# Next block's output projection ahead of a block's last feed-forward group

## The chip, the cores and the metric

The kernel runs on one core of one Trainium2 chip. The metric is the device time of one execution in microseconds (us), lower is better. The engines of the core are PE (TensorE, matrix multiplication, with its weight load PEld), DVE (VectorE), ACT (ScalarE), POOL (GpSimd) and SP (SyncE, which issues nearly all DMAs). Each engine works through its own instructions in order and waits on semaphores for the others.

## What is computed

One decoder layer over 2048 new tokens (one sequence, d_model 1024) and 8 sample tokens with carried states. Two head groups, RWKV-7 and Mamba-2, mix tokens; their outputs, side by side, go through `w_out`; two DeepNorm LayerNorms surround a squared-ReLU feed-forward of width 4096. Cut to the part that the change touches:

```python
proj = x @ w_in                                   # 1024 -> input of both mixers
o_r, wkv_fin = rwkv7_mix(...)                     # 512 columns
o_m, ... = mamba2_mix(...)                        # 512 columns
mix = jnp.concatenate([o_r, o_m], -1) @ w_out     # the output projection
h = layer_norm(ALPHA * x + mix, ln1_g, ln1_b, LN_EPS)
ff = jnp.square(jax.nn.relu(h @ w_ff1)) @ w_ff2
y = layer_norm(ALPHA * h + ff, ln2_g, ln2_b, LN_EPS)
```

Results are float32 within a tight tolerance, so each large product is done as three matmuls on a high and a low half of each factor.

## The kernel before

The 2048 tokens are four blocks of `TB` = 512. First `project` runs x @ w_in for all blocks (to about 760 us), with the mixers of the early blocks beside it. Then `tail(b)` runs once per block, in this order: output projection; first LayerNorm; transposes to `hT` (token columns, feature rows); then 8 groups g of the feed-forward. A group is four `ff1` (one slice f of 128 hidden features each, `LA` = 3 slices run ahead) and 8 units of the second product, one for each half of the output columns (`dh`) and each tile i of 128 tokens. One such unit is 12 matmuls of 512 columns.

A weight piece is made by `wpiece` (L201): SP reads 256 KB into a `wr` tile, ACT rounds it to the high half (L198), DVE or POOL subtracts for the low half (L199). There are 7 `wr` and 8 `w` tiles. `mm3` (L163 to L168) issues the three matmuls: high by high (L166), high by low (L167), low by high (L168). In the traces psb and psa are the four large accumulation banks, psm a small one. The wide tiles (4 KB per partition, names g) hold a block's four h tiles, the hidden slices and the gains; there are 12.

The output projection of a block works in halves of two token tiles. Each half goes through w_out in quarters q of 256 columns; three of four quarters are loaded again for the second half, in turned order, so a block reads 28 pieces. After each bank, L1309 adds it to the residual h, and L1205 takes statistics. `ln` (L1207) finishes the norm: a dozen small DVE instructions, then one ACT instruction per tile (L1222). `gain` multiplies and adds the norm's parameters (L1227, L1228, 128x1024 on DVE). The norm's gains of the first LayerNorm for the transposed copy are folded into L1347, which brings the transposes (`tr`, L173) out of their bank. The first four slices of ff1 (`FIRST`) run over the first 256 tokens while the second half's norm is made.

What a block still owes when its last group ends (second norm, its gains, the store of y) is kept in `late` and stepped by the next block's output projection, two steps per token tile in its second half.

`drive` runs a tail and, for each unit's worth of time that the tail yields, gives a share to fills: the mixers of the next block (`RATE_M` 0.23; with the 8 sample tokens 0.35 in block 0). `before_last(b)`, called when the last group's four ff1 are issued, drains the fills and makes the next tail. That call contains `load_o` (L323), which reads the mixers' output back from DRAM (s_o, 8 pieces of 256 KB) and splits it into `act` tiles. The mixer's last piece, `rwkv_post`, ends in a chain: `inv_root` (a matmul with cst, then DVE), a broadcast through DRAM (d_rs: L552 writes, L554 reads), L786, the read of s_bv (L785), L788, L790, the gate (matmul qsg by gup), L797, and the write of s_o (L798). In before, the last group's units 1 to 7 alternate with the first units of the next projection.

Of the kernel before, what the change touches and what calls it, by code (L numbers as in the profile page):

```python
# [10 lines left out]
F32R = mybir.dt.float32r  # L11
I32 = mybir.dt.int32
AF = mybir.ActivationFunctionType
ALU = mybir.AluOpType
# [13 lines left out]
BUFS = (("wr", 7), ("w", 8), ("act", 8), ("g4", 12), ("r", 2), ("blk", 4),  # L28
        ("m2", 3), ("q2", 2), ("m4", 2), ("ms", 1), ("lr", 1), ("sc", 2), ("ar", 2), ("bk", 1), ("xs", 3),
        ("xf", 1), ("uv", 2), ("bt", 1), ("st", 2), ("r1", 1), ("hids", 8))  # L30
D = 1024
KT = 8
TB = 512
NS = 8
DFF = 4096
NFT = DFF // 128
ALPHA = 2.0 ** 0.25
# [71 lines left out]
class K:  # L109
# [122 lines left out]
    def setup_mix(self):  # L232
# [1045 lines left out]

    def tail(self, b, act, before_last):

        self.pf = "o"
        nc, A = self.nc, self.A
        smp = b == self.sblk
        bs = self.sm("bs", [128, 4, 2, 6], bufs=2)
        W = TB + (NS if smp else 0)
        hs = []
        ln = iter(())
        for half in range(2):
            it = (2 * half, 2 * half + 1)
            tok = smp and half == 1  # L1290
            for q in range(4) if half == 0 else range(3, -1, -1):
                qs = slice(q * 256, (q + 1) * 256)
                if half == 0 or q < 3:
                    wq = [self.wpiece(A["w_out"][q, kp], (2, 256)) for kp in range(4)]
                if len(hs) <= it[0]:
                    for i in it:
                        h = self.wide()
                        nc.sync.dma_start(h, A["x_p"][b * TB + i * 128:b * TB + (i + 1) * 128, :])
                        hs.append(h)
                    if tok:  # L1300
                        xs = self.wide()
                        nc.sync.dma_start(xs[0:8], A["x_s"])
                for i in it:
                    ps = self.bank((128, 256))
                    for k in range(KT):
                        l = [act[k][:, s, i * 128:(i + 1) * 128] for s in range(2)]
                        r = [wq[k // 2][s][:, k % 2, :] for s in range(2)]
                        self.mm3(ps, l, r, k == 0, k == KT - 1)
                    nc.vector.scalar_tensor_tensor(out=hs[i][:, qs], in0=hs[i][:, qs], scalar=ALPHA, in1=ps,  # L1309
                                                   op0=ALU.mult, op1=ALU.add)  # L1310
                    if (q % 2 == 1) != (half == 1):
                        self.stats(hs[i], bs[:, i], q // 2)
                    if half == 1:
                        next(ln, 0)
                        next(self.late, 0)
                    yield 2.6
                if tok:
                    ps = self.bank((128, 256))
                    for k in range(KT):
                        for s in range(2):  # L1320
                            self.mm(ps[0:16], self.osT[:, k, :], wq[k // 2][s][:, k % 2, :],
                                    k == 0 and s == 0, k == KT - 1 and s == 1)
                    nc.scalar.activation(xs[64:80, qs], ps[0:16], AF.Copy)
            for _ in ln:
                pass
            ln = self.ln([hs[i] for i in it], [bs[:, i] for i in it], 128)
            if tok:
                ln = itertools.chain(ln, self.ln_s(xs))
                hs.append(xs)
        for _ in self.late:  # L1330
            pass

        hT = []
        for half in range(2):
            for k in range(KT):
                if half == 0:
                    hT.append(self.sb("act", (128, 2, TB + NS), F32R))
                hl = hT[k]
                p = self.bank((128, 264))
                for i in range(2):  # L1340
                    self.tr(p[:, i * 128:(i + 1) * 128], hs[2 * half + i][:, k * 128:(k + 1) * 128])
                n = 256
                if smp and half == 1:
                    self.tr(p[:, 256:264], hs[4][0:8, k * 128:(k + 1) * 128])
                    n = 264
                raw = self.sb("r", (128, 512))[:, :n]
                nc.scalar.activation(raw, p[:, :n], AF.Identity, scale=self.par("g1", k), bias=self.par("b1", k))  # L1347
                o = 256 * half
                self.split(raw, hl[:, 0, o:o + n], hl[:, 1, o:o + n])
            if half == 0:  # L1350
                first = []
                for f in range(FIRST):
                    first.append(self.ff1(f, hT, [(0, 256)]))
                    next(ln, 0)
                    yield 2.6
                for _ in ln:
                    pass
        self.pf = "f"
        g1 = self.affine(1)
        gain = itertools.chain(*([self.gain(h, 128, *g1) for h in hs[:4]] +  # L1360
                                 ([self.gain(hs[4][0:8], 8, *g1)] if smp else [])))
        segs = [(0, 256), (256, 264)] if smp else [(0, 512)]
        done = {}
        for f in range(FIRST):
            done[f] = self.ff1(f, hT, [(256, W - 256)], first[f])
            next(gain, 0)
            yield 2.6

        def up(f):
            if f < NFT and f not in done:  # L1370
# [3 lines left out]
        nxt = None  # L1374
        for g in range(NFT // 4):
            for f in range(4 * g, 4 * g + 4 + LA):
                if up(f):
                    next(gain, 0)
                    yield 5.2
            for _ in gain:  # L1380
                pass
            hid = [done.pop(f) for f in range(4 * g, 4 * g + 4)]
            last = g == NFT // 4 - 1
            if last:
                nxt = before_last(b)
                self.pf = "f"
                bs = self.sm("bs", [128, 4, 2, 6], bufs=2)
                rows = [A["y_p"][b * TB + i * 128:b * TB + (i + 1) * 128, :] for i in range(4)]
            w2s = []
            order = [(dh, i) for dh in range(2) for i in range(4)]  # L1390
            if last and nxt is None:
                order = [(dh, i) for i in range(4) for dh in range(2)]
            for dh, i in order:
                ds_ = slice(dh * 512, dh * 512 + 512)
                if len(w2s) == dh:
                    w2 = [self.wpiece(A["w_ff2"][f * 128:(f + 1) * 128, ds_], (1, 512)) for f in range(4 * g, 4 * g + 4)]
                    w2s.append(w2)
                    if smp:
                        ps = self.bank()
# [11 lines left out]
                ps = self.bank()  # L1411
                for f in range(4):
                    l = [hid[f][0][:, s, i * 128:(i + 1) * 128] for s in range(2)]
                    r = [w2[f][s][:, 0, :] for s in range(2)]
                    self.mm3(ps, l, r, f == 0, f == 3)
                self.accum(hs[i][:, ds_], ps, g == 0)
                if last:
                    self.stats(hs[i], bs[:, i], dh)
                    if dh == 1 and i == 0:
                        ab = self.affine(2)  # L1420
                    if nxt is None and dh == 1:
                        self.norm(hs[i], bs[:, i], ab, rows[i], POOLN[i])
                    if nxt is not None and 4 * dh + i >= BESIDE:
                        self.pf = "o"
                        yield next(nxt)
                        self.pf = "f"
                yield 2.6

        def finish():
            if nxt is not None:  # L1430
                yield from self.ln(hs[:4], [bs[:, i] for i in range(4)], 128)
# [6 lines left out]
        self.late = finish()  # L1438
        self.nxt = nxt

    def ff1(self, f, hT, segs, hid=None):
# [66 lines left out]
def body(tc, A, nb=4):  # L1508
    with ExitStack() as es:
        k = K(tc, A, nb, es)  # L1510
# [15 lines left out]
        smp = [k.sample(), "s", k.sblk, RATE_S]  # L1526
# [14 lines left out]
        for b in range(nb):  # L1541
# [8 lines left out]
        for _ in k.late:  # L1550
            pass
        k.es2.close()


def layouts(x):

    ac = np.ascontiguousarray
    g = {n: np.asarray(a) for n, a in x.items()}
    d = {}
# [31 lines left out]
    d["w_out"] = ac(g["w_out"][0].reshape(4, 2, 128, 4, 256).transpose(3, 0, 2, 1, 4).reshape(4, 4, 128, 512))  # L1591
# [38 lines left out]
```

## Time and profile before

| what | us |
|---|---|
| median of 3 runs | 2873.99 (2873.67 to 2876.23) |
| profiled execution | 2874.12 |
| its span in the trace | 2872.3 |
| PE busy | 2764.3 (96%) |
| PEld busy | 2280.3 (79%) |
| DVE busy | 2028.7 (71%) |
| ACT busy | 1291.8 (45%) |
| POOL busy | 365.5 (13%) |
| DMA | 395.56 MB, 45.1% of 16 engines on the main queue |

PE is the engine to watch: it is idle for 108 us of the span, and its granted clock is 0.982 of full speed on average. The page's chain of waits that ended last is PE for 73%, DVE for 15% and DMA for 4%. A time lost by another engine counts where PE has to wait for it.

### The profile page before, as it was taken

The numbers are of one execution on the slowest core, as the hardware profiler recorded it, in microseconds if no ns is written. First come the engines' busy times: TensorE is split into PE (matmuls) and PEld (weight loads), VectorE is DVE, ScalarE is ACT, GpSimd is POOL, SyncE is SP. The second block draws the span as 40 slices with busy tenths as digits, with TensorE's granted clock in tenths as the row PEclk, the third lists the DMA queues.
The fourth block names the chain that finished last, engine by engine and source line by source line (L and its number), as shares of the span: only waits on it lengthen the run. The fifth ranks groups of instructions, "written<-read, shape, count | busy, mean of one in ns | idle before, by whom it ended". The sixth has DMA issues, their size and how long they took to land.

```text
span 2872.3 us, 52296 instructions
## 1 busy us (share of the span) xinstructions
PE 2764.3 (96%) x19066; PEld 2280.3 (79%) x19066; DVE 2028.7 (71%) x4809; ACT 1291.8 (45%) x2510; POOL 365.5 (13%) x508
## 2 busy tenths in 40 slices
PE   9998999899989999999899999998999999899997
PEld 7798887677878777778788888887777778888886
DVE  7878969878878776766867667568767656754446
ACT  5554544445527343434544444336344333543432
POOL 2222222212221000002200000022000001200001
PEclk9999999999999999999999999999999999899999
DMA  6655555556644444445434434354443435433231
GB/s 204 190 179 142 174 163 141 166 162 185 197 130 156 126 122 122 136 134 185 144 96 123 121 105 128 92 185 130 125 133 113 115 102 171 151 107 94 86 103 70
DMA packets 333766, 395.56 MB, mean 138 GB/s; under 512 B 84990, under 2 KB 191060, under 8 KB 333500
## 3 DMA queue, kind: packets, MB, share of 16 engines
q1 hardware_dynamic: 333508, 392.22, 45.1%
q8 instruction: 150, 2.46, 0.4%
q14 instruction: 108, 0.88, 0.1%
HBM read 331.34 MB, written 60.81 MB: 137 GB/s over the span
## 4 chain that ended last, share of the span: by engine, by line
PE 73%; DVE 15%; DMA 4%; issue 4%; ACT 2%; SPq 1%; POOL 0%; DVEq 0%; ACTq 0%; POOLq 0%
PE psb L166 17%; PE psb L167 16%; PE psb L168 16%; PE psm L152 6%; PE psa L166 4%; PE psa L167 4%; PE psa L168 4%; DVE w L199 2%; PE psc L152 2%; DVE lr L665 1%; PE psm L173 1%; DVE rX L666 1%; PE psy L751 1%; PE psa L152 1%; DMA wr<-in_w_ff_dram 1%
## 5 line engine op out<-in xcount | busy, mean ns | idle before, releaser
L198 ACT ACTIVATE w<-wr 128x512 fp32r<-128x512 f32 (+1 forms) x836 | 516.5, 626 | 571.7 <-PE psb L168 191.6
L199 DVE TENSOR_TENSOR w<-wr,w 128x512 fp32r<-128x512 f32 x712 | 512.5, 726 | 226.6 <-ACT w L198 221.1
L166 PE MATMUL psb<-act,w 128*128 128x512 f32 (+2 forms) x1768 | 627.3, 356 | 6.4 <-ACT act L198 5.7
L167 PE MATMUL psb<-act,w 128*128 128x512 f32 (+2 forms) x1768 | 620.7, 352 | 0.2 <-DVE act L199 0.2
L168 PE MATMUL psb<-act,w 128*128 128x512 f32 (+2 forms) x1768 | 617.2, 350 | 2.3 <-DVE w L199 2.3
L166 PEld LDWEIGHTS psb<-act,w 128*128 128x128 f32 x1768 | 336.6, 191 | 56.4 <-ACT act L198 5.9
L168 PEld LDWEIGHTS psb<-act,w 128*128 128x128 f32 x1768 | 336.1, 190 | 47.9 <-DVE w L199 2.7
L167 PEld LDWEIGHTS psb<-act,w 128*128 128x128 f32 x1768 | 337.3, 191 | 43.7 <-DVE act L199 1.3
L166 PE MATMUL psb<-w,g 128*128 128x512 f32 x788 | 315.3, 401 | 2.3 <-ACT w L198 1.4
L167 PE MATMUL psb<-w,g 128*128 128x512 f32 x788 | 312.7, 397 | 0.2 <-DVE w L199 0.2
L168 PE MATMUL psb<-w,g 128*128 128x512 f32 x788 | 310.8, 395 | 0.0
L199 POOL TENSOR_TENSOR w<-wr,w 128x512 fp32r<-128x512 f32 x124 | 185.9, 1504 | 530.9 <-ACT w L198 414.6
L1505 DVE TENSOR_TENSOR g<-psb,g 128x512 f32<-128x512 f32 x173 | 118.8, 688 | 148.5 <-PE psb L168 148.1
L166 PEld LDWEIGHTS psb<-w,g 128*128 128x128 f32 x788 | 148.0, 188 | 39.8 <-ACT w L198 2.2
L168 PEld LDWEIGHTS psb<-w,g 128*128 128x128 f32 x788 | 147.9, 188 | 34.3 <-DVE g L199 0.2
L167 PEld LDWEIGHTS psb<-w,g 128*128 128x128 f32 x788 | 148.3, 188 | 33.1 <-DVE w L199 0.5
L199 DVE TENSOR_TENSOR g<-r,g 128x256 fp32r<-128x256 f32 (+1 forms) x172 | 96.7, 562 | 84.6 <-ACT g L198 83.6
L1455 ACT ACTIVATE r<-psb 128x512 f32<-128x512 f32 (+2 forms) x130 | 63.4, 489 | 199.3 <-PE psb L168 197.6
L166 PE MATMUL psa<-act,w 128*128 128x256 f32 (+2 forms) x336 | 115.8, 345 | 0.0
L167 PE MATMUL psa<-act,w 128*128 128x256 f32 (+2 forms) x336 | 114.3, 340 | 0.0
L168 PE MATMUL psa<-act,w 128*128 128x256 f32 (+2 forms) x336 | 113.8, 339 | 0.0
L167 PE MATMUL psb<-w,act 128*128 128x256 f32 x352 | 101.8, 289 | 6.4 <-DVE w L199 5.4
(376 smaller groups left out, 5204.1 us busy)
## 6 DMA issues: line engine op xcount, KB each, us to landing
wr<-in_w_ff_dram SPq DMA_DIRECT2D x512, 256.0 KB
wr<-in_w_in_dram SPq DMA_DIRECT2D x208, 256.0 KB
wr<-in_w_out_dram SPq DMA_DIRECT2D x112, 256.0 KB
lr<-d_l SPq DMA_DIRECT2D x256, 64.0 KB
s_m<-g SPq DMA_DIRECT2D x48, 256.0 KB
ms<-s_m SPq DMA_DIRECT2D x16, 768.0 KB
wr<-in_xT_dram SPq DMA_DIRECT2D x32, 256.0 KB
s_ar<-g SPq DMA_DIRECT2D x16, 512.0 KB
```

Of the source, the lines that this page charges most:

```text
L152: return self.nc.tensor.matmul(out, l, r, start=start, stop=stop)
L166: nc.tensor.matmul(out, l[0], r[0], start=first, stop=False)
L167: nc.tensor.matmul(out, l[0], r[1], start=False, stop=False)
L168: nc.tensor.matmul(out, l[1], r[0], start=False, stop=last)
L173: self.nc.tensor.transpose(out, in_, self.cst[p0:p0 + k, o + p0:o + p0 + k])
L198: nc.scalar.activation(hi, raw, AF.Copy)
L199: (eng or nc.vector).tensor_tensor(out=lo, in0=raw, in1=hi.bitcast(F32), op=ALU.subtract)
L665: nc.vector.tensor_tensor(out=row, in0=X[:, :, s + 1:16], in1=row, op=ALU.mult)
L666: nc.vector.tensor_reduce(X[:, :, s:s + 1], lr[:, :, 17 * s:16 * s + 16], axis=AX.X, op=ALU.add)
L751: acc = lambda o, l, r, start, stop: nc.tensor.matmul(o, l, r, start=start, stop=stop, skip_group_check=True)
L1455: nc.scalar.activation(rl, ps, AF.Relu)
L1505: self.nc.vector.tensor_tensor(out=h, in0=ps, in1=h, op=ALU.add)
```

## The change

- **w_out once.** The projection covers all four token tiles at once, in two halves dh of 512 columns, each in two halves kh of the inner dimension. Four banks stay open over both kh. A block reads 16 pieces instead of 28. The 256-column matmuls of this stage become 512-column ones, and so do the first four ff1 (`FIRST` is gone).
- **Order.** `before_last(b)` stays where it is, but the next tail's whole projection with its norm now runs right behind it, ahead of all 8 units of the last group. The next block's transposes and splits run beside that group's last four units, two feature tiles ahead of each (`TURN`).
- **Late work.** The previous block's second norm, gains and store move from the projection to the first ff1 slices of the next block, two steps per slice, ahead of the first norm's own gains.
- **Buffers.** `LA` 3 to 4, wide tiles 12 to 13.

In block 0 no earlier group exists; there its projection, norm and transposes follow each other directly.

```diff
-FIRST = 4
-BESIDE = 1
-LA = 3
+LA = 4
+TURN = (0, 0, 0, 0, 2, 2, 2, 2)
-BUFS = (("wr", 7), ("w", 8), ("act", 8), ("g4", 12), ...
+BUFS = (("wr", 7), ("w", 8), ("act", 8), ("g4", 13), ...
...
+        for i in range(4):
+            h = self.wide()
+            nc.sync.dma_start(h, A["x_p"][b * TB + i * 128:b * TB + (i + 1) * 128, :])
+            hs.append(h)
...
+        for dh in range(2):
+            ds_ = slice(dh * 512, dh * 512 + 512)
+            pss = []
+            for kh in range(2):
+                ks = range(4 * kh, 4 * kh + 4)
+                wo = [self.wpiece(A["w_out"][k * 128:(k + 1) * 128, ds_], (1, 512)) for k in ks]
+                for i in range(4):
+                    if kh == 0:
+                        pss.append(self.ps("a" if i == 3 else "b"))
+                    for k in ks:
                         l = [act[k][:, s, i * 128:(i + 1) * 128] for s in range(2)]
...
+                        self.mm3(pss[i], l, r, k == 0, k == KT - 1)
+                    if kh:
+                        self.accum(hs[i][:, ds_], pss[i], True)
+                        self.stats(hs[i], bs[:, i], dh)
+                        if dh and i % 2:
+                            for _ in self.ln(hs[i - 1:i + 1], [bs[:, i - 1], bs[:, i]], 128):
+                                pass
                     yield 2.6
...
+        def gains():
+            yield from self.late
+            g1 = self.affine(1)
+            for h in hs[:4]:
+                yield from self.gain(h, 128, *g1)
...
                 if up(f):
+                    next(gain, 0)
                     next(gain, 0)
                     yield 5.2
...
                 nxt = before_last(b)
+                while nxt is not None:
+                    w = next(nxt)
+                    if not w:
+                        break
+                    yield w
...
-            for dh, i in order:
+            for j, (dh, i) in enumerate(order):
+                if last and nxt is not None:
+                    self.pf = "o"
+                    for _ in range(TURN[j]):
+                        next(nxt)
+                    self.pf = "f"
```

Three places, all between blocks 2 and 3, show what moves; rows within one product are left out. First PE before the change, from the last mixer's chain (psm from q and cst, the matmul of `inv_root`) to the first matmul of block 3's projection (psa from w and act). Products of w and g are units of the feed-forward's second matrix, products of act and w are an ff1, qsg by gup is the gate.

```order
L152 MATMUL psm_27062<-q_4291_27019,cst 32x128 x4
L166 MATMUL psa_27093<-act_22712,w_27084 128x512
...
L152 MATMUL psm_27141<-qsg_27139,gup 128x128 x4
L166 MATMUL psb_27168<-w_27150,g_4204_26451 128x512
...
L166 MATMUL psb_27311<-act_22712,w_27302 128x512
...
L166 MATMUL psb_27402<-w_27384,g_4286_26983 128x512
L166 MATMUL psb_27417<-w_27384,g_4286_26983 128x512
L166 MATMUL psb_27483<-w_27384,g_4286_26983 128x512
...
L166 MATMUL psa_27457<-w_27435,act_27343 128x256
```

Between the chain's matmul and the first projection matmul stand two ff1 (24 matmuls each), the eight units of group 6 and three units of group 7. PE after the change, same stretch:

```order
L152 MATMUL psm_26046<-q_4162_26016,cst 32x128 x4
L166 MATMUL psb_26086<-w_26068,g_4004_25069 128x512
...
L166 MATMUL psb_26100<-w_26068,g_4004_25069 128x512
...
L166 MATMUL psa_26132<-w_26068,g_4004_25069 128x512
...
L152 MATMUL psm_26146<-qsg_26130,gup 128x128 x4
L166 MATMUL psb_26153<-w_26068,g_4004_25069 128x512
...
L152 MATMUL psm_29227<-cst,st_25990 64x64 x8
L173 MATMUL psm_29240<-cst,hst 128x128 x4
L166 MATMUL psb_26236<-w_26218,act_26169 128x512
```

Four units of group 6, the gate and two small products are left between them; the eight units of group 7 stand behind the projection. SP before the change, over the same stretch (g from in_x_p is the residual of block 3):

```order
L785 DMA q_4312_27131<-s_bv_77 128x512
L798 DMA s_o_89<-q_4290_27017 128x4x128
L323 DMA wr_27341<-s_o_89 128x512
...
L323 DMA wr_27376<-s_o_89 128x512
L205 DMA wr_27382<-in_w_ff_dram 128x512
...
L205 DMA wr_27433<-in_w_out_dram 128x512
...
L1298 DMA g_4382_27453<-in_x_p_dram 128x1024
```

Four pieces of the feed-forward stand between the reads of s_o and w_out, and the residual comes last. SP after the change:

```order
L1289 DMA g_4204_26210<-in_x_p_dram 128x1024
L1289 DMA g_4205_26212<-in_x_p_dram 128x1024
L785 DMA q_4181_26122<-s_bv_77 128x512
L1289 DMA g_4206_26214<-in_x_p_dram 128x1024
...
L798 DMA s_o_89<-q_4161_26014 128x4x128
L323 DMA wr_26167<-s_o_89 128x512
...
L323 DMA wr_26202<-s_o_89 128x512
L205 DMA wr_26216<-in_w_out_dram 128x512
```

The first piece of w_out follows the eight reads of s_o, and three reads of the residual now stand ahead of the write of s_o, two of them ahead of the read of s_bv. These wait for wide tiles. DVE before the change, in block 3's projection (L1309 brings a bank of the projection to the residual, L1227 and L1228 are block 2's gains):

```order
L1309 SCALAR_TENSOR_TENSOR g_4433_27845<-g_4433_27845,psb_27915 128x256
L1227 TENSOR_TENSOR g_3439_21827<-g_3439_21827,g_4406_27621 128x1024
L1228 TENSOR_TENSOR g_3439_21827<-g_3439_21827,g_4407_27622 128x1024
L1309 SCALAR_TENSOR_TENSOR g_4432_27843<-g_4432_27843,psa_27963 128x256
L1227 TENSOR_TENSOR g_3440_21829<-g_3440_21829,g_4406_27621 128x1024
L1205 BN_STATS obs_27432<-g_4432_27843 128x6
L199 TENSOR_TENSOR w_28032<-wr_28030,w_28032 128x512
L1309 SCALAR_TENSOR_TENSOR g_4433_27845<-g_4433_27845,psb_27992 128x256
L1228 TENSOR_TENSOR g_3440_21829<-g_3440_21829,g_4407_27622 128x1024
```

After the change those gains stand in block 3's first ff1, between splits of hidden slices (g from r) and, behind them, of weights:

```order
L199 TENSOR_TENSOR g_4310_26807<-r_26833,g_4310_26807 128x512
L1227 TENSOR_TENSOR g_3314_20998<-g_3314_20998,g_4313_26838 128x1024
L1227 TENSOR_TENSOR g_3315_21000<-g_3315_21000,g_4313_26838 128x1024
L1228 TENSOR_TENSOR g_3314_20998<-g_3314_20998,g_4314_26839 128x1024
L199 TENSOR_TENSOR g_4324_26875<-r_26901,g_4324_26875 128x512
L1228 TENSOR_TENSOR g_3315_21000<-g_3315_21000,g_4314_26839 128x1024
...
L1228 TENSOR_TENSOR g_3317_21004<-g_3317_21004,g_4314_26839 128x1024
L199 TENSOR_TENSOR w_27052<-wr_27050,w_27052 128x512
```

No bank of the projection waits for them there; the split of the weights for the fifth ff1 stands behind all eight.

## Rows read from the trace of the kernel before

**Rows 1.** Busy time in stretches: engines' busy us, PEclk, DMA share, GB/s.

```profile
796.00:900.00 104.00, 88.97 (x880) 81.27 (x879) 72.47 (x212) 49.70 (x107) 22.14 (x22) 0.93 0.43 132
1276.00:1300.00 24.00, 18.84 (x80) 14.54 (x79) 13.68 (x33) 8.33 (x20) 0.00 (x0) 0.79 0.36 112
1378.00:1446.00 68.00, 59.05 (x464) 48.98 (x463) 53.30 (x102) 37.88 (x83) 17.55 (x13) 0.85 0.41 131
1880.00:1888.00 8.00, 4.94 (x20) 2.44 (x21) 7.40 (x15) 6.63 (x13) 0.53 (x1) 1.00 0.88 279
1944.00:2004.00 60.00, 50.78 (x398) 43.67 (x397) 50.07 (x99) 41.08 (x84) 15.17 (x11) 0.89 0.47 152
2476.00:2520.00 44.00, 33.96 (x226) 31.28 (x226) 27.92 (x56) 27.59 (x63) 4.92 (x3) 0.81 0.31 108
```

**Rows 2.** Waits of PE, 2474 to 2500 us: waiting line, releaser, total us, times, longest.

```profile
PE psa L173 <- DVE g L1309: 3.2, 1, 3.2
PE psb L173 <- DVE g L1309: 3.1, 1, 3.1
```

**Rows 3.** The timeline of DVE from 2477 us: start, us, line, operands, count.

```profile
2475.51 2.32 DVE L1227 TENSOR_TENSOR g<-g,g 128x1024 f32<-128x1024 f32 x1
2478.08 3.42 DVE L1228 TENSOR_TENSOR g<-g,g 128x1024 f32<-128x1024 f32 x2
```

**Rows 4.** Busy time in stretches of 4 us, around that stall.

```profile
2488.00:2492.00 4.00, 3.00 (x12) 2.43 (x13) 2.96 (x14) 3.81 (x9) 0.00 (x0) 0.50 0.95 324
```

**Rows 5.** The timeline of PE at 2384 us, 512 columns, full clock; 25 matmuls apart.

```profile
2383.95 0.39 PE L166 MATMUL psb<-w,g 128*128 128x512 f32 x1
...
2389.73 0.39 PE L167 MATMUL psa<-w,g 128*128 128x512 f32 x1
```

**Rows 6.** The timeline of PE at 1701 us, 256 columns, full clock; 10 matmuls apart.

```profile
1701.32 0.28 PE L167 MATMUL psb<-act,w 128*128 128x256 f32 x1
...
1702.49 0.28 PE L168 MATMUL psb<-act,w 128*128 128x256 f32 x1
```

**Rows 7.** Groups by line and form: count, busy us, mean ns, idle before, releasers.

```profile
L198 ACT ACTIVATE w<-wr 128x512 fp32r<-128x512 f32 x832 | 515.7, 628 | 567.8 <-PE psb L168 187.7 <-PE psa L168 164.0 <-DVE g L1505 106.5
L1228 DVE TENSOR_TENSOR g<-g,g 128x1024 f32<-128x1024 f32 x28 | 38.9, 1393 | 0.1
L1222 ACT ACTIVATE g<-g,onmr,orsy 128x1024 f32<-128x1024 f32 x28 | 33.4, 1234 | 7.6 <-DVE onmr L1218 7.5
L1505 DVE TENSOR_TENSOR g<-psb,g 128x512 f32<-128x512 f32 x173 | 118.8, 688 | 148.5 <-PE psb L168 148.1
L1455 ACT ACTIVATE r<-psb 128x512 f32<-128x512 f32 x63 | 37.7, 599 | 130.6 <-PE psb L168 130.6
```

**Rows 8.** The timeline of PE at 2373 us: the matmul of inv_root.

```profile
2373.56 0.42 PE L152 MATMUL psm<-q,cst 128*32 128x128 f32 x8
```

**Rows 9.** The timeline of SP's DMA issues, 2373 to 2395 us.

```profile
2379.27 1.16 SPq L552 DMA_DIRECT2D d_rs<-rsy  x4
2381.38 1.25 SPq L554 DMA_DIRECT2D q<-d_rs  x2
2387.55 0.35 SPq L785 DMA_DIRECT2D q<-s_bv  x1
2392.37 0.39 SPq L798 DMA_DIRECT2D s_o<-q  x1
2394.68 0.33 SPq L323 DMA_DIRECT2D wr<-s_o  x1
```

**Rows 10.** The timeline of DVE, 2378 to 2393 us.

```profile
2386.84 0.68 DVE L786 TENSOR_TENSOR q<-q,q 128x512 f32<-128x512 f32 x1
```

**Rows 11.** The timeline of ACT, 2386 to 2406 us.

```profile
2403.56 2.73 ACT L198 ACTIVATE act<-wr 128x512 fp32r<-128x512 f32 x4 [12.54 <-PE psb L168]
```

**Rows 12.** The chain of waits, 2474 to 2512 us: landing of a 256 KB piece.

```profile
2474.53 3.53 DMA wr<-in_w_ff_dram
```

**Rows 13.** Waits of PE, 796 to 868 us.

```profile
PE psb L167 <- DVE w L199: 5.4, 1, 5.4
```

More of the change, by code (lines that the diff above doesn't have):

```diff
@@ L1284, in tail @@
         bs = self.sm("bs", [128, 4, 2, 6], bufs=2)
-        W = TB + (NS if smp else 0)
         hs = []
[L1287 to L1305, printed above, removed]
-                        l = [act[k][:, s, i * 128:(i + 1) * 128] for s in range(2)]
[L1307 to L1315, printed above, removed]
@@ L1316, in tail @@
                     yield 2.6
-                if tok:
-                    ps = self.bank((128, 256))
-                    for k in range(KT):
+                if smp:
+                    if kh == 0:
+                        pss.append(self.ps("m"))
+                    for k in ks:
                         for s in range(2):
-                            self.mm(ps[0:16], self.osT[:, k, :], wq[k // 2][s][:, k % 2, :],
+                            self.mm(pss[4][0:16], self.osT[:, k, :], wo[k % 4][s][:, 0, :],
@@ L1322, in tail @@
                                     k == 0 and s == 0, k == KT - 1 and s == 1)
-                    nc.scalar.activation(xs[64:80, qs], ps[0:16], AF.Copy)
-            for _ in ln:
-                pass
[L1326 to L1331, printed above, removed]
-        hT = []
[L1334 to L1357, printed above, removed]
@@ L1358, in tail @@
-        self.pf = "f"
-        g1 = self.affine(1)
-        gain = itertools.chain(*([self.gain(h, 128, *g1) for h in hs[:4]] +
-                                 ([self.gain(hs[4][0:8], 8, *g1)] if smp else [])))
+                    if kh:
+                        nc.scalar.activation(xs[64:80, ds_], pss[4][0:16], AF.Copy)
+        if smp:
+            for _ in self.ln_s(xs):
+                pass
+        yield 0
+        hT = []
+        for k in range(KT):
+            hl = self.sb("act", (128, 2, TB + NS), F32R)
+            hT.append(hl)
+            p = self.bank()
+            for i in range(4):
+                self.tr(p[:, i * 128:(i + 1) * 128], hs[i][:, k * 128:(k + 1) * 128])
+            raw = self.sb("r", (128, 512))
+            nc.scalar.activation(raw, p, AF.Identity, scale=self.par("g1", k), bias=self.par("b1", k))
+            self.split(raw, hl[:, 0, :TB], hl[:, 1, :TB])
+            if smp and k == 1:
+                ph = self.ps("m", (128, KT, NS))
+                for q in range(KT):
+                    self.tr(ph[:, q, :], xs[0:8, q * 128:(q + 1) * 128])
+                xh = self.sm("xsh", [128, KT, NS], bufs=1)
+                for q in range(KT):
+                    nc.scalar.activation(xh[:, q, :], ph[:, q, :], AF.Identity, scale=self.par("g1", q),
+                                         bias=self.par("b1", q))
+            if smp and k:
+                for q in (0, 1) if k == 1 else (k,):
+                    self.split(xh[:, q, :], hT[q][:, 0, TB:], hT[q][:, 1, TB:])
+            yield 0
@@ L1362, in tail @@
+        self.pf = "f"
+        def gains():
[3 more added lines that the diff above has]
+                yield from self.gain(h, 128, *g1)
+            if smp:
+                yield from self.gain(xs[0:8], 8, *g1)
+        gain = gains()
         segs = [(0, 256), (256, 264)] if smp else [(0, 512)]
         done = {}
[L1364 to L1367, printed above, removed]
@@ L1418, in tail @@
                     self.stats(hs[i], bs[:, i], dh)
-                    if dh == 1 and i == 0:
-                        ab = self.affine(2)
                     if nxt is None and dh == 1:
+                        if i == 0:
+                            ab = self.affine(2)
                         self.norm(hs[i], bs[:, i], ab, rows[i], POOLN[i])
[L1423 to L1426, printed above, removed]
                 yield 2.6
@@ L1436, in finish @@
                 yield from self.gain(hs[4][0:8], 8, *ab, A["y_s"])
-        self.late = finish()
+        if nxt is not None:
+            self.late = finish()
         self.nxt = nxt
```

12 lines of the change are left out of this document (8 added, 4 removed).

## Prediction

> **What bounds the kernel now.** I read first the shares of the engines, then the stretches in which PE loses time, then what it waits for there. PE is busy for 96% of the span, so only two things can change the time: the number and width of its matmuls, which this change barely touches, and the stretches where PE stands still or runs at a reduced clock. I count the loss of a stretch as its length less PE's busy time multiplied by the granted clock of the same row [rows 1]. That gives 21.3 us at the start of block 0 (104 - 88.97 x 0.93), 9.1 in the sample's wait at 1276, 17.8 between blocks 0 and 1, 3.1 + 14.8 = 17.9 between blocks 1 and 2, 16.5 between blocks 2 and 3: 82.6 us together. The rest of blocks 0 to 3 has almost none. These are the places where the change works.
>
> What is lost there is seen best between blocks 2 and 3. PE waits twice for L1309 on DVE, the instruction that empties a bank of the output projection, 3.2 and 3.1 us [rows 2]. DVE is late because the gains of block 2 stand ahead of it in its queue: one L1227 of 2.32 us by its bar, then two L1228 that take 3.42 [rows 3]; alone such an instruction takes 1.39 [rows 7]. After these stalls PE's clock is 0.50, half of its full 2.4 GHz, for a slice in which it is already busy for 3.00 of 4 us [rows 4]. So a stall costs its length and some 3 to 6 us behind it at half speed, 4 us on average.
>
> **The change, part by part.**
>
> *Width.* 512 columns issue every 5.78/25 = 0.2312 us [rows 5], 256 columns every 1.17/10 = 0.117 [rows 6]. A pair of halves joined saves 0.0028 us. Per block there are 192 pairs in the projection and 96 in the first four ff1, so the four blocks gain 4 x 288 x 0.0028 = 3.2 us; bounds 0 and 6, since the starts are given to 0.01 us. I take 2.9. The 48 pieces of w_out no longer read cost ACT 0.63 us each [rows 7], off the path except at the junctions.
>
> *Gains and the late norm.* Block by block, eight DVE instructions of 1.39 us, 11 us, leave the projection. Banks there are then emptied at once, and the waits of [rows 2] go. In the first ff1 they stand ahead of the weights' low halves of the fifth slice. Four slices are split before them, 4 x 24 x 0.2312 = 22 us of PE work against 11 us on DVE and a few splits, so I cost them at nothing. If that cover is gone, up to 11 us per block is exposed (third rival).
>
> *Norm and transposes, blocks 1 to 3.* The norm of the last two tiles takes an accumulation (0.69) [rows 7], statistics of about the same, a dozen small DVE instructions, and 2 x 1.23 us on ACT [rows 7], together about 6 us; four units of 12 x 0.2312 = 2.8 us stand over it, 11 us. The transposes of two feature tiles per unit need two copies (0.60) and two high splits (0.63) on ACT [rows 7], 2.5 us in a unit of 2.8, plus the weights' high halves: ACT is slightly late, 2 to 5 us per junction left over.
>
> *Junction 0 to 1.* The mixers of block 1 end long before (the sample's steps follow them), so the read back of s_o is early. By my estimate half of the stretch (a wait on a mixer, the remainder above, some half-speed) stays: 9 instead of 17.8, a gain of 8.8.
>
> *Junctions 1 to 2 and 2 to 3: the s_o chain.* This is what is late next. Before, the matmul of inv_root runs at 2373.56 [rows 8]; the broadcast is written at 2379.27 and read at 2381.38, L786 starts at 2386.84 [rows 10], s_bv is read at 2387.55, s_o written at 2392.37 and read from 2394.68 on [rows 9]: 21.1 us from matmul to first read. It costs nothing there: two ff1 and eleven units lie between (2 x 5.5 + 11 x 2.8 = 42 us), and ACT starts to split these pieces only at 2403.56, after 12.54 us of idleness that PE's products ended, not the DMA [rows 11]. After the change four units (11.1 us) and some 1.4 us of small products lie between, 12.5 us. Behind the first read come a landing of 3.5 us [rows 12] and a high and a low split (0.63 and 0.69), which free the slot for the eighth read; the next slot, 0.7 later, takes the first piece of w_out, which lands after 3.5 and is split in 0.63. First matmul of the projection: 21.1 + 3.5 + 1.3 + 0.7 + 3.5 + 0.6 = 30.7 us after inv_root. Lower bound: DVE is emptier there, so the rsqrt may take 4 us instead of 5.7, L786 follow the broadcast's read by 3.6, and the rest shrink by 0.8: 3.7 us less, 27.0. Between blocks 2 and 3 the read of s_bv also stands behind two reads of the residual, which wait for wide tiles that group 6's last unit still reads; this holds the quick chain at 12.5 us and takes back 2.1. PE therefore stands for 17 to 18 us at block 3. At block 2 only the third of these reads is in the way, and mixer products of block 3 and the sample rows fill 1 to 2 us: 13 to 16. With 4 us at half speed each and the remainders of the norm (4 at block 2, 2 at block 3) I take 22.5 and 23, against 17.9 and 16.5: a loss of 4.6 + 6.5 = 11.1.
>
> The Trainium skill, DMA: Bandwidth & Descriptors, section Rules for kernel authors, says to issue a DMA early, to compute, and to wait for it late. The kernel before does that with s_o, and the changed one issues these reads immediately ahead of their use; by the rule that speaks against the change, and no row here shows the new order. If the cover were still enough, the sum would be that of the first rival.
>
> *Block 0.* No feed-forward group stands over its norm any more. Exposed: 6 us of norm, then the chain of copies and splits, 8 x 1.23 = 9.8 us on ACT against 5.5 us of PE work in the first ff1, with about 2 us until its first piece: 12 to 13, and 4 at half speed. In its place go the waits for w_out: before, 16 pieces are wanted within the first 22 us of the projection, now within 45, and 5.4 us of wait for a weight's low half behind the mixers' small DVE work [rows 13] go in part. Of the 21.3 I count 7 to 8 as waits on the mixers themselves, which stay. 22 to 29, I take 25, a loss of 3.7.
>
> Sum against the profiled 2874.12: -2.9 - 8.8 + 4.6 + 6.5 + 3.7 = +3.1, which is 2877.2. Median and profiled execution differ by 0.13 us, so nothing is added for it. The sample's wait and the kernel's end are not touched.
>
> **The rivals.** *The chain is covered (faster).* If the mixers end two or three units earlier than the order of the program suggests, or the w_out pieces come out in time, stalls at blocks 2 and 3 are 7 us shorter each, with 2 us less at half speed: 2877 - 18 = 2859. For it: the chain has 3.7 us of queueing in it. Against it: the order of the instructions on PE is fixed, and only four units stand there. It decides when the first projection matmul is less than 10 us late.
>
> *Block 0 gains.* If the mixers fill the exposed norm, block 0 falls to 16 instead of 25: 2868, in the forecast's lower edge.
>
> *The gains starve ff1 (slower).* In blocks 1 and 2 the mixers of the next block also use DVE, 71% busy on the whole. If the eight late gains (11 us) plus the eight of the first norm (11 us) outlast the 22 us of prepared weights by a quarter, 5 us per block are lost in blocks 1 and 2 with some half-speed: 2877 + 10 = 2887. It decides when the low half of the fifth slice's weights comes later than the fourth ff1 ends. For it: the gains come in blocks without other work between. Against it: eight w tiles. The slow end of the chain with the upper ends of block 0 lies in the same place.
>
> **How the numbers follow.** This kernel's measurement can tell about 0.2% (5.7 us) from no change: 2868.2 to 2879.7. The forecast, 2877 with 2868 to 2880, has 0.38; the covered chain, 2853 to 2868, 0.27; the slower cases, 2880 to 2897, 0.35. The range leaves about a tenth out on each side: 2860 to 2892.
>
> **What would show it.** Right: PE waits of 13 to 18 us ahead of the first projection matmul of blocks 2 and 3, ended by ACT's split of s_o or of w_out, and no waits of L173 on the projection's accumulation. Wrong: these stalls under 8 us; or waits of L167 for weights in the middle of the ff1 slices; or block 0's loss below 20.

## The result and the profile after

The changed kernel takes 2831.48 us (median of 4 runs, 2827.41 to 2837.96) against 2874.52: ratio 0.9844, 95% interval 0.9829 to 0.9860. That is 43 us faster, where 2877 with 2860 to 2892 was forecast. The profiled execution is the slowest of the four, 2837.96 us with a span of 2836.1; its 36 us less than before are what the trace has to explain.

First the page of the changed kernel: busy time, shares and instructions of each engine, then the chain of waits by engine and the two costliest groups.

```profile
PE 2739.1 (97%) x17978; PEld 2211.4 (78%) x17978; DVE 1990.6 (70%) x4733; ACT 1246.6 (44%) x2376; POOL 297.0 (10%) x468
...
PE 66%; DVE 5%; DMA 3%; issue 1%; ACT 1%; SPq 0%; POOL 0%; DVEq 0%; ACTq 0%; POOLq 0%
...
L198 ACT ACTIVATE w<-wr 128x512 fp32r<-128x512 f32 x788 | 485.5, 626 | 637.9 <-PE psb L168 396.2
L199 DVE TENSOR_TENSOR w<-wr,w 128x512 fp32r<-128x512 f32 x704 | 491.3, 705 | 252.9 <-ACT w L198 248.9
```

The shares of the chain add up to 76%, since this chain can be followed back only to 699 us, and that of before to the start; so DVE's 5% does not compare with the 15% of before. Behind 700 us DVE's part of the chain falls from 214 to 132 us. DVE's own busy time hardly moves (2028.7 to 1990.6). ACT's weight splits, 832 of this form in [rows 7] and 4 of another, are 788 now: the 48 pieces of w_out.

The stretches that answer to [rows 1], in the view of busy time in stretches (length; busy us of PE, PEld, DVE, ACT, POOL; granted clock; DMA share; GB/s). They are the start of block 0, the sample's wait, junction 0 to 1, junction 1 to 2 in two parts, junction 2 to 3 in two parts:

```profile
787.00:934.00 147.00, 137.66 (x998) 105.86 (x996) 111.16 (x296) 62.90 (x114) 15.68 (x17) 0.95 0.43 130
1276.00:1300.00 24.00, 19.05 (x92) 14.71 (x91) 16.49 (x39) 10.53 (x21) 2.62 (x2) 0.86 0.45 144
1300.00:1447.00 147.00, 145.82 (x920) 121.95 (x919) 106.49 (x247) 76.92 (x168) 18.82 (x12) 1.00 0.43 144
1840.00:1876.00 36.00, 27.12 (x132) 21.19 (x131) 21.72 (x39) 12.02 (x22) 4.59 (x4) 0.76 0.64 212
1876.00:1997.00 121.00, 120.49 (x572) 94.34 (x570) 86.23 (x197) 61.82 (x102) 12.01 (x11) 1.00 0.47 148
2364.00:2400.00 36.00, 16.54 (x78) 12.34 (x78) 14.14 (x19) 12.30 (x21) 5.55 (x4) 0.72 0.72 224
2400.00:2509.00 109.00, 109.00 (x489) 88.71 (x488) 74.10 (x140) 53.91 (x84) 5.81 (x4) 1.00 0.40 130
```

By the measure of the prediction (length less PE's busy time at the granted clock, summed over slices of 4 us, since the clock differs inside a stretch) they lose 14.9, 7.3, 1.2, 15.9 and 22.4 us. Junction 0 to 1 has lost nearly all its stalls; the whole norm, transposes and first ff1 at junction 2 to 3 run with PE busy 109.00 of 109 us. In their place PE stands still ahead of each of the last two projections. At block 3 it is one wait; PE's longest from 2340 to 2420 us, the matmul of `inv_root`, and SP's DMA issues behind it:

```profile
PE psb L166 <- ACT w L198: 18.9, 1, 18.9
```

```profile
2358.26 0.43 PE L152 MATMUL psm<-q,cst 128*32 128x128 f32 x8
```

```profile
2363.27 1.15 SPq L552 DMA_DIRECT2D d_rs<-rsy  x4
2365.41 1.24 SPq L554 DMA_DIRECT2D q<-d_rs  x2
2368.88 1.74 SPq L1289 DMA_DIRECT2D g<-in_x_p_dram  x2
2370.72 0.37 SPq L785 DMA_DIRECT2D q<-s_bv  x1
...
2377.72 0.38 SPq L798 DMA_DIRECT2D s_o<-q  x1
2380.10 4.68 SPq L323 DMA_DIRECT2D wr<-s_o  x8
2385.84 14.19 SPq L205 DMA_DIRECT2D wr<-in_w_out_dram  x15
```

The reader finds the prediction's chain link by link: 21.8 us from the matmul to the first read of s_o, 5.7 to the first piece of w_out, which ends PE's wait at 2391.68, 33.4 us after the matmul (30.7 was forecast). Two links are longer. From the read of s_bv to the write of s_o it takes 7.0 us, where before took 4.8 [rows 9]: the read stands behind two reads of the residual, and the chain of waits from 2350 to 2400 us shows it in the queue for 5.44 us. And the first piece of w_out takes 5.13 us to land instead of 3.5:

```profile
2370.72 5.44 DMA q<-s_bv
2376.28 0.70 DVE q L790
2377.01 0.70 DVE q L797
2377.72 2.29 DMA s_o<-q
...
2380.78 3.65 DMA wr<-s_o
...
2385.84 5.13 DMA wr<-in_w_out_dram
2391.00 0.64 ACT w L198
2391.68 0.79 PE psb L166
```

At block 2 the chain is as long, 33.2 us from the matmul of `inv_root` at 1837.40 to the first matmul of the projection at 1870.56, but it is not one stall. PE's waits from 1840 to 1880 us:

```profile
PE psm L152 <- issue: 3.7, 1, 3.7
PE psb L166 <- ACT w L198: 2.3, 1, 2.3
PE psm L152 <- DVE m L844: 1.8, 1, 1.8
PE psm L173 <- DVE sc L646: 0.7, 1, 0.7
```

Only 2.3 us end with the split of w_out. Small mixer products stand between the last unit and the projection, and run for some 10 us; the first of them starts at 1855.52, just after L797 has read the gate's bank (1855.42), and the waits on L844 and L646 lie between them. With a last 0.2 us PE stands still for 8.7 us.

### The profile page after: what moved, and what is told of

Its sections match the earlier page's. It is cut to its first block, busy times and chain, and to the rows that moved or that the text cites. A ratio compares the mean times of both kernels' runs of the same rounds, so it can differ in the third digit from the quotient of the medians.

```text
span 2836.1 us, 49575 instructions
## 1 busy us (share of the span) xinstructions
PE 2739.1 (97%) x17978; PEld 2211.4 (78%) x17978; DVE 1990.6 (70%) x4733; ACT 1246.6 (44%) x2376; POOL 297.0 (10%) x468
## 4 chain that ended last, share of the span: by engine, by line
PE 66%; DVE 5%; DMA 3%; issue 1%; ACT 1%; SPq 0%; POOL 0%; DVEq 0%; ACTq 0%; POOLq 0%
PE psb L166 14%; PE psb L167 14%; PE psb L168 14%; PE psm L152 5%; PE psa L166 4%; PE psa L167 4%; PE psa L168 4%; PE psc L152 2%; PE psm L173 1%; PE psy L751 1%; PE psb L152 1%; DMA wr<-in_w_out_dram 1%; DMA q<-s_bv 0%; DMA g<-in_ln_g_dram 0%; DVE g L1228 0%
## 5 line engine op out<-in xcount | busy, mean ns | idle before, releaser
L198 ACT ACTIVATE w<-wr 128x512 fp32r<-128x512 f32 x788 | 485.5, 626 | 637.9 <-PE psb L168 396.2
L199 DVE TENSOR_TENSOR w<-wr,w 128x512 fp32r<-128x512 f32 x704 | 491.3, 705 | 252.9 <-ACT w L198 248.9
L166 PE MATMUL psb<-act,w 128*128 128x512 f32 (+2 forms) x1688 | 612.4, 363 | 6.8 <-ACT act L198 5.8
L167 PE MATMUL psb<-act,w 128*128 128x512 f32 (+2 forms) x1688 | 605.9, 359 | 0.0
L168 PE MATMUL psb<-act,w 128*128 128x512 f32 (+2 forms) x1688 | 603.3, 357 | 2.1 <-DVE w L199 2.1
L166 PEld LDWEIGHTS psb<-act,w 128*128 128x128 f32 x1688 | 319.6, 189 | 60.1 <-ACT act L198 5.8
L168 PEld LDWEIGHTS psb<-act,w 128*128 128x128 f32 x1688 | 319.2, 189 | 51.3 <-DVE w L199 2.5
L167 PEld LDWEIGHTS psb<-act,w 128*128 128x128 f32 x1688 | 320.0, 190 | 47.0 <-DVE act L199 0.9
L166 PE MATMUL psb<-w,g 128*128 128x512 f32 x768 | 310.0, 404 | 1.0 <-DVE g L1510 1.0
L167 PE MATMUL psb<-w,g 128*128 128x512 f32 x768 | 305.5, 398 | 0.0
L168 PE MATMUL psb<-w,g 128*128 128x512 f32 x768 | 304.6, 397 | 0.0
L166 PEld LDWEIGHTS psb<-w,g 128*128 128x128 f32 x768 | 144.7, 188 | 38.7 <-issue 2.0
L199 POOL TENSOR_TENSOR w<-wr,w 128x512 fp32r<-128x512 f32 x84 | 118.3, 1409 | 538.8 <-ACT w L198 256.4
L168 PEld LDWEIGHTS psb<-w,g 128*128 128x128 f32 x768 | 144.8, 189 | 33.7 <-issue 0.2
L167 PEld LDWEIGHTS psb<-w,g 128*128 128x128 f32 x768 | 144.9, 189 | 32.2 <-issue 0.4
L199 DVE TENSOR_TENSOR g<-r,g 128x512 fp32r<-128x512 f32 (+1 forms) x160 | 92.5, 579 | 57.1 <-ACT g L198 56.7
L166 PE MATMUL psa<-act,w 128*128 128x512 f32 (+1 forms) x320 | 114.1, 357 | 0.0
L167 PE MATMUL psa<-act,w 128*128 128x512 f32 (+1 forms) x320 | 112.6, 352 | 0.0
L168 PE MATMUL psa<-act,w 128*128 128x512 f32 (+1 forms) x320 | 112.4, 351 | 0.0
L166 PE MATMUL psb<-g,w 128*128 128x256 f32 (+2 forms) x312 | 105.4, 338 | 0.3 <-ACT g L578 0.3
```

The lines of the kernel that those rows point to most:

```text
L166: nc.tensor.matmul(out, l[0], r[0], start=first, stop=False)
L167: nc.tensor.matmul(out, l[0], r[1], start=False, stop=False)
L168: nc.tensor.matmul(out, l[1], r[0], start=False, stop=last)
L198: nc.scalar.activation(hi, raw, AF.Copy)
L199: (eng or nc.vector).tensor_tensor(out=lo, in0=raw, in1=hi.bitcast(F32), op=ALU.subtract)
```

## The experiments

Where did the gain come from, if the foreseen stall is there, at block 3 in full? My first theory (G) was the place of the gains in DVE's queue; its rival (O) was that the new order pays, by setting a feed-forward group over norm and transposes. Later rivals were the pieces of w_out and the buffers. Ratios stand against runs of the kernel before on the same chip.

### The s_o chain: e3_rate, e7_before_rate, e8_rate28

```diff
-RATE_M0, RATE_M, RATE_S = 0.2, 0.23, 0.35
+RATE_M0, RATE_M, RATE_S = 0.2, 0.25, 0.35
```

on the changed kernel (e3_rate), on the kernel before (e7_before_rate), and 0.28 on the changed kernel (e8_rate28).

> The changed kernel with the mixers' share of the drive raised from 0.23 to 0.25, so that the mixers of blocks 2 and 3 end some 28 units of the drive's time earlier, and the chain to s_o with them; nothing else differs. If the s_o chain is what PE waits for ahead of the projections of blocks 2 and 3 (18.9 us, and about 8, and half-speed behind both), both stalls go: 2831 - 25 to -32, about 2802. The rival, that the denser mixers cost DVE and PE elsewhere what they give back here: 2825 or more.

> A control for e3_rate: the kernel before with the mixers' share raised from 0.23 to 0.25 in the same way. There the s_o chain has the last group's units over it, so if e3_rate's 29 us are the s_o stalls, nothing changes: 2871 to 2877. If an earlier end of the mixers pays by itself, 2860 or less.

> The changed kernel with the mixers' share at 0.28 instead of the 0.25 of e3_rate. If the chain is covered at 0.25 already, nothing is left to win: 2798 to 2806. If a part of it still lies open (block 3 loses 7.5 us in e3_rate's trace), 2790 to 2797. If denser mixers crowd DVE in the ff1 stages, 2808 or more.

e3_rate: 2802.54 us, ratio 0.9760 (0.9740 to 0.9780). e7_before_rate: 2870.40, 0.9992 (0.9978 to 1.0005), no change. e8_rate28: 2796.76, 0.9733 (0.9711 to 0.9755), which lies in the range given for a chain still partly open. But in e3_rate's trace PE waits neither for s_o nor for w_out at the two junctions; some 6 us are lost at 2152 to 2168 us, where mixer products wait for ACT (L710). So the chain is covered at 0.25 already, and what 0.28 gains on top, 6 us, is at the edge of what these runs can tell apart.

An earlier end of the mixers is thus worth 29 us at 0.25 and 35 at 0.28 where the projection waits for s_o (24 and 32 by the ratios, since the runs are from different chips), and nothing where it doesn't: at 0.25 in the kernel before, at 0.28 in e9_order_rate below. The stalls are the s_o chain, and it costs the change some 30 us. In e8_rate28 the first read of s_o for block 3 is issued 37 us ahead of the projection, in the changed kernel 11.6:

```profile
2314.56 14.31 SPq L323 DMA_DIRECT2D wr<-s_o  x8
```

```profile
2351.55 0.39 PE L166 MATMUL psb<-w,act 128*128 128x512 f32 x1
```

Both junctions are without a gap there. Its busy time in stretches, from ahead of the projection to the first group of blocks 2 and 3:

```profile
1830.00:1975.00 145.00, 145.00 (x742) 113.87 (x741) 100.05 (x220) 68.35 (x112) 19.35 (x14) 1.00 0.43 144
2340.00:2466.00 126.00, 126.00 (x562) 102.47 (x561) 80.23 (x147) 57.57 (x90) 11.53 (x8) 1.00 0.41 136
```

This version beats both kernels, by 77 and by 35 us.

### The order: e2_order, e9_order_rate

```diff
                 nxt = before_last(b)
-                while nxt is not None:
-                    w = next(nxt)
-                    if not w:
-                        break
-                    yield w
...
-                if last and nxt is not None:
-                    self.pf = "o"
-                    for _ in range(TURN[j]):
-                        next(nxt)
-                    self.pf = "f"
```

on the changed kernel; e9_order_rate has the share 0.28 as well.

> The changed kernel with its order undone: the last feed-forward group runs first, then the next block's projection, norm and transposes follow one another with no group over them; w_out in 16 pieces, full-width stages and the late gains in ff1 stay. The read back of s_o then has eight units over it. Theory O: norm and transposes lie open at three junctions, as in block 0, 15 us each and some half-speed, while the stalls on s_o (19 us at the last junction, 8 at the one before, with half-speed 32 together) go: 2831 + 50 - 32 = 2849. Theory G: the open norm is small against the s_o stalls, 2831 - 15 = 2816 or less.

> e2_order (projection, norm and transposes behind the last group) with the mixers' share at 0.28 as in e8_rate28, so that the two differ by the order alone, with the s_o chain covered in both. If the order's worth is the open norm and transposes (e2_order loses 21.5, 11.6 and 12.2 us at the three junctions, e8_rate28 9.8, 2.8 and 2.4), this one stays at 2824 to 2834 and the order is worth about 30 us once the chain is covered. If the share itself gives time, 2815 or less, and the order is worth under 20.

e2_order: 2829.09 us, 0.9850 (0.9831 to 0.9869), the same as the changed kernel. e9_order_rate: 2835.58, 0.9868 (0.9852 to 0.9884). So the order, as shipped, gives nothing: what it hides of norm and transposes it loses to s_o. With the chain covered it is worth 39 us (e9_order_rate against e8_rate28), or 32 against e2_order, the faster of the two without the order. Both theories missed e2_order's number, O by 20 us and G by 13. And 45 us of gain stand without the order. PE's waits in e9_order_rate between blocks 2 and 3 (2380 to 2500 us) show what the order takes away, the open norm of L1222 and the copies of the transposes:

```profile
PE psb L173 <- ACT g L1222: 4.3, 3, 2.0
PE psb L166 <- ACT r L1337: 1.5, 1, 1.5
PE psa L173 <- ACT r L1337: 0.9, 1, 0.9
```

### The gains: e1_gains, e5_late

Both are the kernel before with the late norm and gains stepped in ff1, and with 13 wide tiles. e1_gains steps them ahead of the first half-width ff1 (the two lines at its name below are in it alone), e5_late in the second round of halves, of which it has three instead of four:

```diff
                     if half == 1:
                         next(ln, 0)
-                        next(self.late, 0)
...
-        for _ in self.late:
-            pass
...
                 for f in range(FIRST):
+                    for _ in range(3):             # e1_gains
+                        next(self.late, 0)
                     first.append(self.ff1(f, hT, [(0, 256)]))
...
+        def gains():                               # then the first norm's gains
+            yield from self.late
...
             done[f] = self.ff1(f, hT, [(256, W - 256)], first[f])
             next(gain, 0)
+            next(gain, 0)                          # e5_late: three steps each, FIRST = 3
...
```

> The kernel before with one part of the change: the previous block's second norm and gains leave the output projection and are stepped in the first four half-width ff1 of the next block, three steps ahead of each; the order of the blocks, w_out in 28 pieces and the half-width stages stay. Theory G (the gains on DVE's queue ahead of the projection's banks are most of what the junctions lose): the waits on L1309 go at three junctions, about 10 us each with the half-speed behind them, so 2874.5 - 25 to -30, about 2847, and the rest of the change brings the remaining 15. Theory O (the order, which sets a feed-forward group over norm and transposes, is what pays): the waits only move, from L1309 to the split of weights or to the norm, so 2866 to 2874.

> The kernel before with the late norm and gains moved further than in e1_gains: they are stepped in the second half-width round of ff1 (three slices instead of four run in halves, so that the wide tiles suffice), and on DVE they now stand behind the first eight transposes' splits of the next block instead of between the projection's accumulations. Order, 28 pieces and halves stay. Theory G (the gains in DVE's queue): the waits of the transposes on L1309 go, 2874 - 25 = 2849. Theory W (16 pieces and stages of full width give the 45 us of e2_order): only those 6 to 8 us of L1309 and half-speed change, 2862 to 2872.

e1_gains: 2869.29 us, 0.9985 (0.9976 to 0.9995). Taken alone this speaks against G, but DVE's timeline from 2470 us shows that the edit did not do what it says:

```profile
2470.26 1.21 DVE L1228 TENSOR_TENSOR g<-g,g 128x1024 f32<-128x1024 f32 x1
2471.40 0.41 DVE L1309 SCALAR_TENSOR_TENSOR g<-g,psb 128x256 f32<-128x256 f32 x1
2471.73 1.98 DVE L1228 TENSOR_TENSOR g<-g,g 128x1024 f32<-128x1024 f32 x1
...
2476.26 3.42 DVE L1227 TENSOR_TENSOR g<-g,g 128x1024 f32<-128x1024 f32 x2
2479.60 0.41 DVE L1309 SCALAR_TENSOR_TENSOR g<-g,psa 128x256 f32<-128x256 f32 x1
```

The gains still stand between the accumulations of L1309, as in [rows 3]: a scheduler fixes each engine's order, and a later line did not make a later place. By what rule it placed them is not shown. In e5_late the first L1227 at this junction comes 20 us after the last L1309:

```profile
2464.39 0.41 DVE L1309 SCALAR_TENSOR_TENSOR g<-g,psb 128x256 f32<-128x256 f32 x1
...
2484.61 1.22 DVE L1227 TENSOR_TENSOR g<-g,g 128x1024 f32<-128x1024 f32 x1
```

It takes 2847.35 us, 0.9913 (0.9889 to 0.9937): 25 us, the number of theory G. PE's waits on L1309 behind 760 us fit: 13.7 us in before, 13.9 in e1_gains, 1.9 in e5_late. Between blocks 2 and 3 (2440 to 2510 us) one is left, where [rows 2] has two of over 3 us:

```profile
PE psb L173 <- DVE g L1309: 0.9, 1, 0.9
```

The 13 wide tiles stand in e1_gains too, which is 4 us faster than before; three slices in halves were not tried alone, so a share of theirs in the 25 us is not ruled out.

### Pieces and buffers: e6_pieces, e13_before_la, e14_order_la, e4_la, e12_la28

e6_pieces makes 12 further pieces per block in e2_order and uses none of them:

```diff
                 wo = [self.wpiece(A["w_out"][k * 128:(k + 1) * 128, ds_], (1, 512)) for k in ks]
+                for k in ks[:3]:
+                    self.wpiece(A["w_out"][k * 128:(k + 1) * 128, ds_], (1, 512))
```

The other four set `LA`, always with 13 wide tiles: 4 in the kernel before (e13_before_la), 3 in e2_order (e14_order_la), in the changed kernel (e4_la) and in e8_rate28 (e12_la28).

> e2_order with 12 further pieces of w_out per block read, rounded and subtracted without use, so 28 per block as in the kernel before; PE's work is the same. If the 48 pieces less (0.63 us of ACT and 0.73 of DVE or 1.5 of POOL each, and 12 MB of reads) are what brings e2_order down, 2829 + 20 to 30, about 2855. If it is the width of the stages and the place of the gains, 2829 to 2835.

> The kernel before with ff1 four slices ahead and 13 wide tiles, nothing else changed: the buffers' part of the change alone. If the fourth slice pays by itself, as e12_la28 (25 us lost without it) suggests, 2874 - 15 to -25, about 2855. If it pays only where projection and last group stand in the new order, 2868 to 2877.

> e2_order with ff1 three slices ahead: pieces, width and gains of the change without the order and without the fourth slice. If the fourth slice is worth something only beside the new order, 2826 to 2833, as e2_order. If it is part of e2_order's 45 us, 2838 or more.

> The changed kernel with ff1 three slices ahead instead of four; nothing else differs. If the fourth slice only shifts work between groups, the time is the same within 4 us (2827 to 2836). If it covers the late gains or the s_o chain (the last group's ff1 are done one slice earlier, and one unit's worth of cover stands elsewhere), 2838 or more.

> e8_rate28 with ff1 three slices ahead instead of four, so that the s_o chain, which made e4_la hard to read, is covered in both. If the fourth slice had only been cover for the chain, 2794 to 2800, as e8_rate28. If it pays in the ff1 stages (the weights' splits behind eight gains), 2803 or more.

| kernel | us | ratio (interval) | against | difference |
|---|---|---|---|---|
| e6_pieces | 2843.40 | 0.9898 (0.9869 to 0.9927) | e2_order | +14 |
| e13_before_la | 2857.59 | 0.9951 (0.9936 to 0.9966) | before | -16 |
| e14_order_la | 2846.43 | 0.9904 (0.9888 to 0.9921) | e2_order | +17 |
| e4_la | 2839.13 | 0.9879 (0.9859 to 0.9898) | changed | +8 |
| e12_la28 | 2821.41 | 0.9821 (0.9805 to 0.9838) | e8_rate28 | +25 |

The 48 pieces are worth 14 us, half of the 20 to 30 that one theory gave and clear of the other. In the profiled execution of e6_pieces PE loses 20, 15 and 12 us at the three junctions, in that of e2_order 12, 10 and 12. Whether it is ACT's time, DVE's, POOL's or the reads was not separated. The fourth slice, which I had not priced, is worth 16 us by itself; e14_order_la, which keeps the 13 wide tiles, loses 17 without it. What it moves shows in ACT's timeline of e13_before_la, ahead of block 3's projection, which starts at 2399.98 there:

```profile
2382.60 0.63 ACT L198 ACTIVATE act<-wr 128x512 fp32r<-128x512 f32 x1 [6.64 <-DMA wr<-s_o]
2383.65 0.63 ACT L198 ACTIVATE act<-wr 128x512 fp32r<-128x512 f32 x1 [0.41 <-DMA wr<-s_o]
2385.86 3.85 ACT L198 ACTIVATE act<-wr 128x512 fp32r<-128x512 f32 x6 [1.58 <-DMA wr<-s_o]
```

In [rows 11] ACT waits for PE before it can split s_o, at 2403.56, 13 us ahead of the projection; here DMA ends the wait, 17 us ahead: the last ff1 of the block, which reads the act tiles that the splits need, runs one group earlier. That this is all that the slice brings is not shown. Why e12_la28 loses 25 and e4_la only 8 stays open. In e12_la28's trace 7.5 us are lost ahead of block 2's projection, in waits of mixer products for DVE (L646, L844) and not for s_o.

### A miss: e10_sample

```diff
-RATE_M0, RATE_M, RATE_S = 0.2, 0.28, 0.35
+RATE_M0, RATE_M, RATE_S = 0.2, 0.28, 0.45
```

> e8_rate28 with the share of block 0's fills, the mixers of block 1 and the sample's steps, raised from 0.35 to 0.45. The wait of PE on the read of d_y, 5 us and some half-speed in every trace at about 1280 us, belongs to a chain through DRAM in the sample's steps that the drain at the end of the block runs into. If an earlier end of these steps sets matmuls over it, 2797 - 6 to -9, about 2789. If the wait stands wherever the steps stand, or the denser fills crowd DVE, 2795 or more.

2806.40 us, 0.9769 (0.9754 to 0.9784): 10 us slower than e8_rate28. The wait on d_y stays (3.8 us), and from 800 to 1152 us, in block 0, PE loses 25 us where e8_rate28 loses 14.

## Why the prediction was wrong

It forecast no change, since a stall that it saw was to eat what the junctions won. The stall came; most of the gains had no term in the sum, or one too small. Of its own signs, the stall of block 3 and the absence of waits of L173 on the projection's accumulation came as named for right; block 0's loss under 20 came as named for wrong, and block 2 shows neither: 8.7 us of waits, 2.3 of them ended by the split.

- **s_o chain, right.** 18.9 us of wait at block 3 against 17 to 18 forecast. By the whole junction (half-speed included) 22.4 us against 23, and 15.9 at block 2 against 22.5. There PE stands still for 8.7 us, not 13 to 16, because mixer products run for some 10 us inside the chain, where 1 to 2 were allowed. The controls and the cover show that the chain costs the change some 30 us. The rival in which the chain is covered was the right thing to look for; it shortened the stalls by 18 us, and covering them whole gives more. The Trainium skill's rule (DMA: Bandwidth & Descriptors, section Rules for kernel authors) to issue early and wait late is borne out in e8_rate28, where the same reads are issued 37 us ahead of their use instead of 11.6 and PE does not wait.
- **"Off the path except at the junctions", wrong.** The 48 pieces had a price of nothing. They cost 14 us (e6_pieces), most of it at the first two junctions. The sentence named the exception and then left it out of the sum.
- **Buffers, not priced.** The fourth slice was listed as part of the change and no term was made for it: 16 us alone (e13_before_la).
- **Gains, mis-sized.** I allowed them 8.8 us, at junction 0 to 1 together with the norm, and let the s_o stall swallow the rest. Alone they give 25 us (e5_late, with the reservation above).
- **Norm and transposes, mis-sized.** 2 to 5 us per junction were to be left over because ACT is slightly late. PE is busy for 109.00 of 109 us behind the stall at junction 2 to 3: nothing is left over, and junction 0 to 1 loses 1.2 us instead of 9. The order's cover is worth 32 to 39 us once s_o is covered.
- **Block 0, mis-sized.** 25 us forecast, 14.9 measured. The waits on the norm (L1222) are 4.3 us instead of 6, those on the copies behind it (L1337) 2.0 instead of some 6, and those on mixer products, 7 to 8 in the forecast, 2.9. The rival that block 0 gains has the size right, 16, but not the reason: between the last two waits on L1222 PE has only transposes, and the norm lies open there.
- **Width, nearly right.** 2.9 us forecast. At full clock the projection's matmuls take 119 ns from start to start in halves and 233 joined, on average, so 1536 x 0.119 - 768 x 0.233 = 4 us, and 1 to 2 for the ff1.
- **The base was too small.** I took PE's busy time as work. Of the 36 us between the profiled executions, 20 are lost time; 17 are busy time at full clock (2728 to 2711, over slices of 4 us), of which joined halves are some 5. The 192 transposes give some 4 more: at full clock and without a gap their starts lie 131 ns apart in before and 107 after, on average, with 109 in the median of both. The ends of matmuls are modelled in the profile, so that a short wait can count as busy. Where the rest of the 17 us lies is not shown. The 82.6 us that I had to give out were not all that could be won.

The parts don't add: 25 for the gains, 14 for the pieces, 16 for the fourth slice and 5 for the width are 60, and without the order all together give 45 (e2_order). They overlap: with the fourth slice alone (e13_before_la) PE's waits on L1309 fall from 13.7 to 8.1 us already, with the gains alone to 1.9.

## What to carry to other kernels

Before a stall is set against a gain, ask of each the same question: what is it worth if the other were not there. Here the order is worth 32 to 39 us and its own new wait some 30, and one number in the drive, the share of the fills, decides whether they cancel. A change with four parts needs a term for each, the buffers too, and work "off the critical path" is free only where the engine that does it is not the one waited for.

## What was not expected of the hardware

PE's busy time in a profile is not all work: of the 128-column transposes that ran at full clock without a gap in the records, a quarter lie 165 ns or more apart in before, and after the change nine in ten 110 or less. A read of 256 KB issued behind two reads of 512 KB took 5.44 us to land, behind one of them, at block 2, 3.68, and one among other reads of 256 KB 3.53 [rows 12].
